# Two products in strict turn, and new start addresses for one half of the weights: a float32 decoder on one Trainium2 core

## The chip, the cores and the metric

The kernel runs on one core of a Trainium2 chip. The metric is the device time of one execution in microseconds. TensorE multiplies, VectorE and ScalarE prepare weights and finish results, GpSimd adds a few tensors, SyncE issues the transfers.

## The reference

Two layers; each takes a sequence of 256 positions by 2048 channels. Cut to the products that matter:

```python
h = jnp.einsum('bsd,dc->bsc', x, w_in)          # 12,288 columns for two branches, 12 + 4,096 for gates
out_a = dilated_mixture(rope(qa), rope(ka), va)  # 12 heads of 128
up_a = jnp.einsum('bsw,wd->bsd', out_a * jax.nn.silu(za), w_up_a)
out_b = forgetting_attention(qb, kb, vb, log_f)  # 12 heads of 128
up_b = jnp.einsum('bsw,wd->bsd', out_b * jax.nn.silu(zb), w_up_b)
g_a, g_b = sigmoid(g_logit + b_gate)             # 2 x 2048 columns
y = jnp.einsum('bsd,de->bse', g_a * up_a + g_b * up_b, w_out)
x = layer_norm(DEEPNORM_ALPHA * x + y, ln_g, ln_b)
```

All is float32. Nearly all arithmetic is in the products with `w_in`, `w_up_a`, `w_up_b` and `w_out`.

## The kernel before

**Split products.** A float32 operand is split into a high part, rounded by ScalarE to the shorter format `float32r`, and a low part, the rest, which VectorE subtracts (`split`, lines 69 and 70). A product is then high x high + high x low + low x high. Activations lie as tiles [128, 2, 256]: for each 128 channels the high part of the 256 positions and behind it the low part. Where the weights stand still in TensorE (`stat_mm`), one 128 x 128 weight tile needs two products:

- a *wide* one, line 164: the weights' high part stands, and 512 columns move (activations high and low), into both halves of a PSUM tile;
- a *narrow* one, line 162: the weights' low part stands, and 256 columns move (activations high).

`fold` adds the two halves of the PSUM tile later. Each product has a weight load of its own, which TensorE makes while the product before it streams. Products for V (`v_mm`, lines 353 and 355) are the other way round: activations stand, 512 and then 256 columns of weights move.

**Units, pieces and order.** A `Unit` is one column block of 128 (or 256 for V) over all 16 or 12 blocks of channels; it is cut into `Piece`s of eight or six such blocks (four for V). `prep` loads a piece's weights, takes one of six buffers `w` and splits into it; it is called four pieces ahead (`prep_to(done + 4)`). `run(i, part)` issues one product, `part` 0 wide and 1 narrow. The loop at the end of `trunk` goes through the pieces in a fixed order: at the start of each layer four units go side by side (five pieces each in the first layer, two in the second), in all other places a piece at a time. In a single piece all wide products come first and then all narrow ones; side by side it is two wide, two narrow. Between units the products of the attention are put in, at fixed places.

**Addresses.** A buffer `w` has 2,240 float32 per partition (8,960 bytes, 35 times 256) and starts at a multiple of 256 bytes, as the activations do. Of 128-wide weights the high part starts 48 elements in and the low part 1,088 elements behind it, so both lie at 192 modulo 256 bytes; a weight tile is 512 bytes a partition, which keeps that. V's weights start 16 elements in, at 64.

`keep_warm` (line 139) is a product of zeros, put in where TensorE has to wait for the layer norm; its weights are the first 128 columns of what it streams.

Of the kernel before, what the change touches and what calls it, by code (L numbers as in the profile page):

```python
# [32 lines left out]
SCALE = HD ** -0.5  # L33

SLOT = KT // 4 * (NV + HEADS)

W_PART = (SLOT + 63) // 64 * 64
W_OFF = 48
V_OFF = 16
# [3 lines left out]
def trunk(ctx: ExitStack, tc: tile.TileContext, xt, w_st, w_v, w_vf, w_up, w_o,  # L43
          b_f, b_g, ln_g, ln_b, rope_c, bias_a, mask_c, ident_c, yt):
    nc = tc.nc
# [17 lines left out]
    def load_raw(ap, n):  # L63
        t = wp.tile([128, SLOT], F32, name="raw", tag="raw", bufs=7)
        nc.sync.dma_start(t[:, :n], ap)
        return t[:, :n]

    def split(hi, lo, src):
        nc.scalar.activation(hi, src, AF.Copy)  # L69
        nc.vector.tensor_tensor(lo, src, hi.bitcast(F32), op=ALU.subtract)  # L70

    class Piece:
# [6 lines left out]
        def prep(self):  # L79
            n = len(self.kts) * self.w  # L80
            raw = load_raw(self.ap, n)
            t = wp.tile([128, 2 * W_PART + 64], F32R, name="w", tag="w", bufs=6)
            o = W_OFF if self.w == 128 else V_OFF
            self.t = t[:, o:o + 2 * W_PART].rearrange("p (a b) -> p a b", a=2)
            split(self.t[:, 0, :n], self.t[:, 1, :n], raw)

        def run(self, i, part):
            s = slice(i * self.w, (i + 1) * self.w)
            self.unit.mm(self.kts[i], self.t[:, :, s], part)

    class Unit:

# [63 lines left out]
    def stat_mm(acts, ps, kt_n, halves=2):  # L156

        def mm(kt, w, part):
            a = acts(kt)
            first, last, o = kt == 0, kt == kt_n - 1, ps()[:, :S]  # L160
            if part == 1:
                nc.tensor.matmul(o, w[:, 1], a[:, 0], start=False, stop=last)  # L162
            elif halves == 2:
                nc.tensor.matmul(ps(), w[:, 0], a, start=first, stop=False)  # L164
            else:
                nc.tensor.matmul(o, w[:, 0], a[:, 0], start=first, stop=False)
                nc.tensor.matmul(o, w[:, 0], a[:, 1], start=False, stop=False)
        return mm

    def fold(dst, ps, scale=1.0):  # L170
# [460 lines left out]
    n = 0  # L631
# [9 lines left out]
    def prep_to(n):  # L641
        nonlocal started
        while started < min(n, len(todo)):
            p = todo[started]
            if p.unit is units[0]:
                load_x(p.kts[0], 2)
            p.prep()
            if p.unit is units[SIDE - 1] and len(p.kts) > 2:
                load_x(p.kts[2], 2)
            started += 1  # L650
            if started == SIDE * len(units[0].pieces) + 1:
                load_rope()
            if started == SIDE * len(units[0].pieces) + 4:
                load_consts()

    done = 0
    for g in order:
        done += len(g)
        n = number[id(g[0].unit)]
        if g[0].first and n in norms:  # L660

            stats, apply = norms[n]
            stats()
            stages = [apply(j2, j2 < 2) for j2 in range(KT // 2)]
            run = [stages[0][0], stages[0][1], stages[1][0]]
            for j2 in range(2, KT // 2):
                run += [stages[j2][0], stages[j2 - 1][1]]
            run.append(stages[-1][1])
            ins = None
            for i, f in enumerate(run):  # L670
                if i == 9:
                    with tc.issue_after(ins.ins):
                        prep_to(done + 2)
                if ins is None:
                    ins = f()
                else:
                    with tc.issue_after(ins.ins):
                        ins = f()
        prep_to(done + 4)
        for p in g:  # L680
            if p.first:
                for f in jobs.get(number[id(p.unit)], []):
                    f()
                if p.unit.before:
                    p.unit.before()
        if len(g) > 1:
            for i in range(0, len(g[0].kts), 2):
                for p in g:
                    for part in range(2):
                        p.run(i, part)  # L690
                        p.run(i + 1, part)
        else:

            for part in range(2):
                for i in range(len(g[0].kts)):
                    g[0].run(i, part)
        for p in g:
            if p.last and p.unit.after:
                p.unit.after()
# [87 lines left out]
```

## Time and profile before

| | |
|---|---|
| median of 3 runs | 1979.7 us (1979.55 to 1981.81) |
| the profiled execution | 1979.52 us |
| its span, first to last instruction | 1977.7 us |
| mean granted TensorE clock | 0.996 of 2.4 GHz |
| TensorE products busy | 99% of the span |
| VectorE, ScalarE, GpSimd busy | 64%, 50%, 4% |
| transfers | 362.74 MB, mean 183 GB/s |

A record of a product is longer than the distance from its start to the next one's, since products are pipelined. So a row with eight products in it is read by its start and the next row's start, and a mean duration is compared with other durations only.

### The profile page before, as it was taken

Reading aid. Unit: us, or ns where it says so; the run is one execution under the profiler, and the core shown is the slowest. Engines: PE = TensorE matmul, PEld = TensorE weight load, DVE = VectorE, ACT = ScalarE, POOL = GpSimd, SP = SyncE. Lnnn points to the kernel's source line nnn. Section 1 sums busy time; section 2 is a strip of 40 time slices with the busy share of each in tenths; the row PEclk is TensorE's granted clock in tenths of the full one; section 3 lists DMA queues with packets and bytes.
Section 4 is the critical chain, followed back from the end, with each engine's and each line's share of the span. In section 5 each row is a group of like instructions: output and inputs, shape, how many; then the busy total and the mean of one; then the engine's idle time right before and its main releaser. Section 6 shows DMA issues by size and latency. Waiting matters only on the chain.

```text
span 1977.7 us, 29731 instructions
## 1 busy us (share of the span) xinstructions
PE 1957.8 (99%) x11449; PEld 1727.2 (87%) x11449; DVE 1269.8 (64%) x1908; ACT 987.3 (50%) x1558; POOL 69.5 (4%) x64
## 2 busy tenths in 40 slices
PE   9999999999999999999999999999999999999997
PEld 7888888889888888888888888888898888888886
DVE  7666665555555555668787666655555555556686
ACT  6444444444544445555465444445454444445544
POOL 0000000001000000001100000000010000000022
PEclk9999999999999999999999999999999999999998
DMA  9655555666656556665555555556666665556651
GB/s 307 204 180 179 172 169 172 192 197 211 185 178 183 179 170 180 183 202 192 160 181 171 179 176 178 166 181 185 203 203 185 185 179 179 170 174 191 210 184 64
DMA packets 108630, 362.74 MB, mean 183 GB/s; under 512 B 12464, under 2 KB 15944, under 8 KB 108488
## 3 DMA queue, kind: packets, MB, share of 16 engines
q1 hardware_dynamic: 107320, 357.42, 58.5%
q0 software_dynamic: 1024, 3.17, 0.7%
q8 instruction: 89, 1.46, 0.3%
q14 instruction: 53, 0.43, 0.1%
q10 hardware_dynamic: 144, 0.26, 0.1%
HBM read 358.68 MB, written 2.12 MB: 182 GB/s over the span
## 4 chain that ended last, share of the span: by engine, by line
PE 98%; DVE 1%; DMA 0%; ACT 0%; issue 0%; DVEq 0%; ACTq 0%
PE mm L164 53%; PE mm L162 27%; PE mm L353 8%; PE mm L355 4%; PE ps_s L258 1%; PE po L287 1%; PE pt L278 1%; PE po L288 1%; PE ps_s L257 1%; PE mm L351 0%; PE mm L348 0%; PE mm L349 0%; DMA xraw<-xt 0%; DVE gated L566 0%; DMA raw<-w_st 0%
## 5 line engine op out<-in xcount | busy, mean ns | idle before, releaser
L70 DVE TENSOR_TENSOR w<-raw,w 128x1024 fp32r<-128x1024 f32 (+3 forms) x716 | 840.5, 1178 | 443.5 <-ACT w L69 442.1
L69 ACT ACTIVATE w<-raw 128x1024 fp32r<-128x1024 f32 (+3 forms) x716 | 717.9, 1004 | 455.5 <-issue 222.6
L164 PE MATMUL mm<-x,w 128*128 128x512 f32 x3328 | 851.2, 396 | 6.4 <-DVE x L589 3.1
L164 PEld LDWEIGHTS mm<-x,w 128*128 128x128 f32 x3328 | 594.3, 188 | 109.9 <-ACT x L577 2.7
L162 PEld LDWEIGHTS mm<-x,w 128*128 128x128 f32 x3328 | 454.0, 188 | 39.2 <-DVE w L70 1.4
L162 PE MATMUL mm<-x,w 128*128 128x256 f32 x3328 | 463.8, 279 | 0.0
L173 ACT ACTIVATE c<-mm 128x256 f32<-128x256 f32 x320 | 120.3, 384 | 456.2 <-PE mm L162 422.5
L175 DVE TENSOR_TENSOR p<-mm,c 128x256 f32<-128x256 f32 x252 | 106.8, 425 | 186.9 <-ACT c L173 186.4
L164 PE MATMUL mm<-gated,w 128*128 128x512 f32 x768 | 196.6, 391 | 0.0
L353 PE MATMUL mm<-w,x 128*128 128x512 f32 x704 | 176.7, 393 | 0.0
L164 PEld LDWEIGHTS mm<-gated,w 128*128 128x128 f32 x768 | 135.3, 188 | 21.1
L353 PEld LDWEIGHTS mm<-w,x 128*128 128x128 f32 x704 | 126.1, 188 | 22.7
L164 PE MATMUL mm<-merged,w 128*128 128x512 f32 x480 | 120.1, 392 | 0.0
L162 PEld LDWEIGHTS mm<-gated,w 128*128 128x128 f32 x768 | 108.3, 188 | 10.4
L162 PE MATMUL mm<-gated,w 128*128 128x256 f32 x768 | 111.2, 279 | 0.0
L355 PEld LDWEIGHTS mm<-w,x 128*128 128x128 f32 x704 | 94.7, 188 | 7.4
L164 PEld LDWEIGHTS mm<-merged,w 128*128 128x128 f32 x480 | 86.0, 188 | 15.5 <-DVE merged L70 0.5
L355 PE MATMUL mm<-w,x 128*128 128x256 f32 x704 | 96.5, 279 | 0.0
L162 PEld LDWEIGHTS mm<-merged,w 128*128 128x128 f32 x512 | 68.1, 188 | 4.8
L162 PE MATMUL mm<-merged,w 128*128 128x256 f32 x512 | 69.9, 279 | 0.0
L447 POOL TENSOR_TENSOR u<-x 128x512 f32<-128x512 f32 x16 | 31.7, 1982 | 603.9 <-DVE merged L70 242.4
L267 ACT ACTIVATE z<-z,s 128x128 f32<-128x128 f32 x96 | 42.3, 444 | 0.0
(128 smaller groups left out, 910.9 us busy)
## 6 DMA issues: line engine op xcount, KB each, us to landing
raw<-w_st SPq DMA_DIRECT2D x408, 512.0 KB, 3.9
raw<-w_up SPq DMA_DIRECT2D x128, 384.0 KB, 3.1
raw<-w_v SPq DMA_DIRECT2D x88, 512.0 KB, 4.4
raw<-w_o SPq DMA_DIRECT2D x64, 512.0 KB, 4.1
raw<-w_vf SPq DMA_DIRECT2D x8, 536.0 KB, 4.4
raw<-w_st SPq DMA_DIRECT2D x12, 256.0 KB, 5.6
nb<-cum POOLq DMA_DIRECT2D x12, 256.0 KB, 4.5
yt<-gated SPq DMA_DIRECT2D x8, 256.0 KB, 2.1
```

The source lines that it names most:

```text
L69: nc.scalar.activation(hi, src, AF.Copy)
L70: nc.vector.tensor_tensor(lo, src, hi.bitcast(F32), op=ALU.subtract)
L162: nc.tensor.matmul(o, w[:, 1], a[:, 0], start=False, stop=last)
L164: nc.tensor.matmul(ps(), w[:, 0], a, start=first, stop=False)
L173: nc.scalar.activation(c, ps[:, S:], AF.Copy, scale=scale)
L175: nc.vector.tensor_tensor(dst, ps[:, :S], c, op=ALU.add)
L257: nc.tensor.matmul(ps[:, 0], q[:, :128], k[:, :128], start=True, stop=True)
L258: nc.tensor.matmul(ps[:, 1:3].rearrange("p a b -> p (a b)"), q[:, 128:], k, start=True, stop=True)
L267: nc.scalar.activation(z[:, sl], z[:, sl], AF.Exp, scale=-1.0, bias=s4[:, c:c + 1], accum_out=s4[:, 2 + c:3 + c])
L353: nc.tensor.matmul(o, xh, w, start=first, stop=False)
L355: nc.tensor.matmul(o[:, :NV], xl, w[:, 0], start=False, stop=last)
L447: nc.gpsimd.tensor_tensor(u, x[:, :, 0], x[:, :, 1], op=ALU.add)
```

## The change

Two things change for weights that stand still. The order within a piece: after each wide product comes the narrow one of the same weights, in single pieces and where four units go side by side. And the addresses: the high part stays at 48 elements (192 modulo 256 bytes), the low part starts at element 1,088 of the buffer (0 modulo 256 bytes) and no longer at 1,136. V's products keep order and addresses.

```diff
@@ Piece @@
             t = wp.tile([128, 2 * W_PART + 64], F32R, name="w", tag="w", bufs=6)
-            o = W_OFF if self.w == 128 else V_OFF
-            self.t = t[:, o:o + 2 * W_PART].rearrange("p (a b) -> p a b", a=2)
-            split(self.t[:, 0, :n], self.t[:, 1, :n], raw)
+            if self.w == 128:
+                self.parts = t[:, W_OFF:W_OFF + n], t[:, W_PART:W_PART + n]
+                split(*self.parts, raw)
+            else:
+                self.t = t[:, V_OFF:V_OFF + 2 * W_PART].rearrange("p (a b) -> p a b", a=2)
+                split(self.t[:, 0, :n], self.t[:, 1, :n], raw)
 
         def run(self, i, part):
             s = slice(i * self.w, (i + 1) * self.w)
-            self.unit.mm(self.kts[i], self.t[:, :, s], part)
+            w = [p[:, s] for p in self.parts] if self.w == 128 else self.t[:, :, s]
+            self.unit.mm(self.kts[i], w, part)
@@ the loop over the pieces @@
             for i in range(0, len(g[0].kts), 2):
                 for p in g:
-                    for part in range(2):
-                        p.run(i, part)
-                        p.run(i + 1, part)
+                    for j in (i, i + 1):
+                        for part in range(2):
+                            p.run(j, part)
         else:
 
-            for part in range(2):
-                for i in range(len(g[0].kts)):
-                    g[0].run(i, part)
+            n = range(len(g[0].kts))
+            for i, part in ([(i, part) for i in n for part in range(2)] if g[0].w == 128 else
+                            [(i, part) for part in range(2) for i in n]):
+                g[0].run(i, part)
```

In `stat_mm`, `w[:, 0]` and `w[:, 1]` become `w[0]` and `w[1]`; the products are the same.

On TensorE, in the second layer, a single piece of eight channel blocks that follows the scores of a head stands like this before (x_81 to x_84 are the activations of two blocks each; 128x512 is a wide product, 128x256 a narrow one):

```order
L258 MATMUL ps_s<-k,q 128x256
L164 MATMUL mm<-x_81,w 128x512 x2
L164 MATMUL mm<-x_82,w 128x512 x2
L164 MATMUL mm<-x_83,w 128x512 x2
L164 MATMUL mm<-x_84,w 128x512 x2
L162 MATMUL mm<-x_81,w 128x256 x2
L162 MATMUL mm<-x_82,w 128x256 x2
L162 MATMUL mm<-x_83,w 128x256 x2
L162 MATMUL mm<-x_84,w 128x256 x2
```

The first eight products of the same piece after the change (lines 164 and 162 are now 169 and 167):

```order
L263 MATMUL ps_s<-k,q 128x256
L169 MATMUL mm<-x_81,w 128x512
L167 MATMUL mm<-x_81,w 128x256
L169 MATMUL mm<-x_81,w 128x512
L167 MATMUL mm<-x_81,w 128x256
L169 MATMUL mm<-x_82,w 128x512
L167 MATMUL mm<-x_82,w 128x256
L169 MATMUL mm<-x_82,w 128x512
L167 MATMUL mm<-x_82,w 128x256
```

The first narrow product moved from the ninth place of the piece to the second, and each kind now stands behind the other.

Where four units go side by side, at the start of the second layer behind the last product of `keep_warm`, TensorE has before:

```order
L139 MATMUL pw<-warm 128x512
L164 MATMUL mm<-x_81,w 128x512 x3
L162 MATMUL mm<-x_81,w 128x256 x2
L164 MATMUL mm<-x_81,w 128x512
L162 MATMUL mm<-x_81,w 128x256 x2
L164 MATMUL mm<-x_81,w 128x512 x2
L162 MATMUL mm<-x_81,w 128x256 x2
```

and after the change:

```order
L144 MATMUL pw<-warm 128x512
L169 MATMUL mm<-x_81,w 128x512
L167 MATMUL mm<-x_81,w 128x256
L169 MATMUL mm<-x_81,w 128x512
L167 MATMUL mm<-x_81,w 128x256
L169 MATMUL mm<-x_81,w 128x512
L167 MATMUL mm<-x_81,w 128x256
```

Here the first narrow product moved from behind three wide ones to behind one. On VectorE, GpSimd and SyncE nothing moved; on ScalarE one split of weights stands one place earlier, ahead of one fold.

## Rows read from the trace of the kernel before

**Rows 1.** The page: busy time by engine, and the last chain's shares by line.

```profile
PE 1957.8 (99%) x11449; PEld 1727.2 (87%) x11449; DVE 1269.8 (64%) x1908; ACT 987.3 (50%) x1558; POOL 69.5 (4%) x64
...
PE mm L164 53%; PE mm L162 27%; PE mm L353 8%; PE mm L355 4%; PE ps_s L258 1%; PE po L287 1%; PE pt L278 1%; PE po L288 1%; PE ps_s L257 1%; PE mm L351 0%; PE mm L348 0%; PE mm L349 0%; DMA xraw<-xt 0%; DVE gated L566 0%; DMA raw<-w_st 0%
```

**Rows 2.** L164, L162: span, PE, PEld, clock, DMA; by source: duration min/median/max ns.

```profile
0.00:1977.80 1977.80, 1167.81 (x4576) 815.50 (x4576) 1.00 0.60 183
...
0.00:1977.80 1977.80, 644.99 (x4608) 630.43 (x4608) 1.00 0.60 183
...
L353 PE MATMUL mm<-w,x x704: 388/394/398, 35.3 to 1703.0; 128*128 128x512 f32 x176
...
L355 PE MATMUL mm<-w,x x704: 276/279/283, 37.2 to 1704.0; 128*128 128x256 f32 x176
```

**Rows 3.** Timeline of TensorE, 790 to 826 us: start, length, line, shape, count.

```profile
790.45 2.00 PE L164 MATMUL mm<-x,w 128*128 128x512 f32 x8
792.28 1.07 PE L162 MATMUL mm<-x,w 128*128 128x256 f32 x8
793.19 1.99 PE L164 MATMUL mm<-x,w 128*128 128x512 f32 x8
795.01 1.11 PE L162 MATMUL mm<-x,w 128*128 128x256 f32 x8
795.96 1.53 PE L164 MATMUL mm<-gated,w 128*128 128x512 f32 x6
...
798.04 1.53 PE L164 MATMUL mm<-gated,w 128*128 128x512 f32 x6
...
823.63 2.00 PE L164 MATMUL mm<-x,w 128*128 128x512 f32 x8
```

**Rows 4.** Groups of TensorE by line, 792.60 to 793.10 us: busy us, mean ns.

```profile
L162 PE MATMUL mm<-x,w 128*128 128x256 f32 x7 | 1.0, 276 | 0.0
```

**Rows 5.** The same, where a narrow run begins: at 792.33, 795.06, 758.69 us.

```profile
L164 PE MATMUL mm<-x,w 128*128 128x512 f32 x1 | 0.4, 394 | 0.0
L162 PE MATMUL mm<-x,w 128*128 128x256 f32 x1 | 0.3, 276 | 0.0
...
L164 PE MATMUL mm<-x,w 128*128 128x512 f32 x1 | 0.4, 392 | 0.0
L162 PE MATMUL mm<-x,w 128*128 128x256 f32 x1 | 0.3, 283 | 0.0
...
L164 PE MATMUL mm<-gated,w 128*128 128x512 f32 x1 | 0.4, 388 | 0.0
L162 PE MATMUL mm<-gated,w 128*128 128x256 f32 x1 | 0.3, 279 | 0.0
```

**Rows 6.** The same, where a wide run begins: at 793.21 and 796.00 us.

```profile
L162 PE MATMUL mm<-x,w 128*128 128x256 f32 x2 | 0.4, 276 | 0.0
L164 PE MATMUL mm<-x,w 128*128 128x512 f32 x1 | 0.4, 388 | 0.0
...
L162 PE MATMUL mm<-x,w 128*128 128x256 f32 x2 | 0.4, 280 | 0.0
L164 PE MATMUL mm<-gated,w 128*128 128x512 f32 x1 | 0.4, 392 | 0.0
```

**Rows 7.** The same, ahead of V's products: at 709.40 and 709.68 us.

```profile
L162 PE MATMUL mm<-x,w 128*128 128x256 f32 x3 | 0.5, 279 | 0.0
...
L353 PE MATMUL mm<-w,x 128*128 128x512 f32 x1 | 0.4, 396 | 0.0
L162 PE MATMUL mm<-x,w 128*128 128x256 f32 x1 | 0.3, 277 | 0.0
```

**Rows 8.** The same, of keep_warm at 980.30 us.

```profile
L139 PE MATMUL pw<-warm 128*128 128x512 f32 x1 | 0.4, 398 | 0.0
```

**Rows 9.** Waits of PEld and of ACT: us in total, times, longest.

```profile
PEld mm L162 <- DVE w L70: 1.4, 4, 0.4
...
ACT w L69 <- PE mm L162: 104.8, 98, 2.7
```

More of the change, by code (lines that the diff above doesn't have):

```diff
@@ L161, in mm @@
             if part == 1:
-                nc.tensor.matmul(o, w[:, 1], a[:, 0], start=False, stop=last)
+                nc.tensor.matmul(o, w[1], a[:, 0], start=False, stop=last)
             elif halves == 2:
-                nc.tensor.matmul(ps(), w[:, 0], a, start=first, stop=False)
+                nc.tensor.matmul(ps(), w[0], a, start=first, stop=False)
             else:
-                nc.tensor.matmul(o, w[:, 0], a[:, 0], start=first, stop=False)
-                nc.tensor.matmul(o, w[:, 0], a[:, 1], start=False, stop=False)
+                nc.tensor.matmul(o, w[0], a[:, 0], start=first, stop=False)
+                nc.tensor.matmul(o, w[0], a[:, 1], start=False, stop=False)
         return mm
```

## The prediction

> **What bounds the kernel now.** I read the page from the top. TensorE's matmul row is busy 1957.8 of 1977.7 us and its weight-load row 1727.2 us, while VectorE is at 64% and ScalarE at 50%; in the chain that ended last line 164 (the wide products) holds 53% of the span and line 162 (the narrow ones) 27% [rows 1]. So what counts is the distance from one product's start to the next one's, and nothing else unless TensorE is made to wait. The sums by line then say how many products there are: 4,576 wide and 4,608 narrow with weights standing still, and 704 of each in the products with moving weights, which the change leaves as they are [rows 2].
>
> A busy TensorE need not be at its peak, so I read distances next, from the starts of runs in a stretch without attention [rows 3]. From 790.45 to 823.63 us there are six pieces of 8 + 8 and eight of 6 + 6 products, 96 pairs in 33.18 us: **345.6 ns for a pair** of one wide and one narrow product. The reader is to see in the same rows that runs of eight narrow products come in two lengths: 792.28 to 793.19 is 0.91 us, 113.8 ns each, and 795.01 to 795.96 is 0.95 us, 118.8 ns each. Wide runs take 1.83 us, 228.8 ns each. The granted clock is 1.00 of 2.4 GHz in the mean [rows 2], at which 512 and 256 columns would stream in 213.3 and 106.7 ns, so each product carries 7 to 16 ns on top.
>
> The records' durations show this more finely than starts to 10 ns: the seven narrow records of the fast run have a mean of 276 ns [rows 4], so a narrow record is some 162.5 ns longer than the distance it stands for (276 against 113.8, rounded), and a wide one 163 (392 [rows 5] against 228.8). With weights standing still I find wide records of 388, 392 and 394 ns [rows 5]; where weights move, wide ones go from 388 to 398 and narrow ones from 276 to 283 [rows 2]. In distances: wide 225.5 to 235.5, narrow 113.5 to 120.5.
>
> Which of these levels a product takes is handed on by the product before it. Behind a wide of 394 ns the first narrow takes 276; behind one of 392 it takes 283; behind one of 388 it takes 279 [rows 5]. Behind a narrow of 276 the first wide takes 388, behind one of 280 it takes 392 [rows 6]. In between, a narrow run keeps its level, as the mean of the seven shows [rows 4].
>
> **The change, part by part.** *Removed and added work:* none. Products, loads, splits and transfers are the same in number and size; each product's weight load still runs under the product before it.
>
> *The order.* Before, of the 16 loads of a piece of eight, seven high and one low part are loaded under wide products, seven low and one high (the next piece's) under narrow ones. After, every low part is loaded under a wide product and every high part under a narrow one, and each wide is followed by a narrow and the reverse. So what [rows 5, 6] show decides at every product and no longer once in eight. With the loads at the addresses of before, I can walk the chain from those rows: narrow 276, wide 388, narrow 279, wide 392, narrow 283, and then wide 392 and narrow 283 again and again, if a 283 hands on what a 280 does. That is (392 - 163) + (283 - 162.5) = 349.5 ns a pair, 3.9 more than now. The order by itself is worth 4,576 x 3.9 = +17.8 us.
>
> *The addresses.* The activations start at 0 modulo 256 bytes, high and low parts both at 192 before; now the low part starts at 0. It is the part that is loaded under the wide product. A load at 0 under a wide product of this kind is in no row. The nearest rows: at the start of a unit with moving weights the activations become the loaded operand, at 0, under the last narrow product. That product takes 277 ns at two such places (566.7 and 709.5 us), where the three before it at the second have a mean of 279 [rows 7]: two ns faster, so the position of a load counts, and 0 is better there, though the wide product behind it is one of 396 [rows 7]. The other row goes against it: a keep-warm product, 512 columns wide, whose next load has the same start as its moving operand takes 398 [rows 8], the slowest level, but it stands right behind a restart and the load reads the very bytes that it streams. The bounds of the wide product are then 388 and 398 ns, so the pair lies between 225.5 + 113.5 = 339.0 and 235.5 + 120.5 = 356.0 ns: from -30.2 to +47.6 us over 4,576 pairs.
>
> I take the narrow row as nearer (the same activations, in mid-stream) and let it bring the wide to within 1.5 ns of its fastest level: 227 ns. A wide a little above 388 must then leave its narrow at 276 and not at 279, which would repeat itself: 227 + 113.5 = 340.5 ns, 5.1 less than now. That is 4,576 x 5.1 = **-23.3 us**.
>
> The Trainium skill speaks against this term ("SBUF — State Buffer", section on two separate sides): it gives TensorE ports of its own that wait for nobody, with a second independent read port for weight loads, so that no start address would matter. The narrow record of 277 disagrees; by the rule this term would be 0.
>
> *Low parts needed sooner.* In a single piece the first low product comes seven wides (1.6 us) earlier, in the groups of four units one wide (0.23 us) earlier. In the single pieces this is hidden: ScalarE's split waited 98 times on a narrow product of TensorE [rows 9], that is for one of the six weight buffers to come free, so splits are done pieces ahead, and a piece is 2.1 to 2.8 us long [rows 3]. Were that cover gone, every piece would pay 1.6 us. In the groups of four the cover is thin: weight loads of line 162 waited four times for VectorE's low part, 1.4 us together [rows 9]. Each of the four pays up to 0.23 us more: +0.9 us. At most all 20 + 8 pieces of such groups pay it, 6.4 us. One split moves ahead of one fold on ScalarE in the first group; both have slack, nothing.
>
> *Sum.* The profiled execution took 1979.5 us (span 1977.7), the median of the three runs is 1979.7. 1979.5 - 23.3 + 0.9 = **1957.1 us**. VectorE, ScalarE and the transfers would go up by 1% of their shares and stay covered.
>
> **Rivals.**
> *The address does nothing for the wide product, the order does its part (slower).* Place: every pair. For it: the walk through [rows 5, 6], whose loads all lie at 192, ends in the slow pair, and the one wide product with an aligned load is slow [rows 8]. Against it: the 277 ns records. Price +17.8 + 0.9: 1998 us. It decides once the narrow product behind a wide keeps to 283 and not to 276; with a wide at 394 on top it would be 1979.5 + 4,576 x 6.4 + 0.9 = 2010.
> *Neither matters.* Place: every pair again, if fast and slow levels keep taking turns as they do now. For it: in the mean over 96 pairs all levels come up, in runs of six as in runs of eight [rows 3]. Against it: the levels are not random, one follows from the one before [rows 5, 6], and a strict turn has one way from each. Price 0 to +0.9: 1980 us. By the rule of the Trainium skill's page on SBUF above, it would go this way too.
> *Half a gain.* Two levels take turns, as 340.5 and 345.6: 343 ns, 1968.5 us. It counts with my forecast.
>
> **How the numbers follow.** The forecast with the half gain has 0.56, the slower rival 0.28, no change 0.16. The forecast's own range is 1949 (the lower bound, 1979.5 - 30.2) to 1970. The range for 8 in 10 must hold the middle case and most of the slower one: 1949 to 1998. A measurement of this kernel tells about 0.2% (4 us) from no change: faster 0.56, same 0.16, slower 0.28.
>
> **What would show it.** The same stretch would hold its 96 pairs in 32.7 us (340.5 ns) and not 33.18. Narrow records of the line that was 162 would have 276 to 277 as median and wide ones 388 to 390; 283 and 392 would show the slower rival, 279 and 392 the neutral one. Products with moving weights must stay at 393 and 279 ns, or something else moved. In the first 18 us, waits of weight loads for VectorE would be more than four, and over 2.3 us together if the groups of four pay. I am wrong if the levels are set by something that the load's address doesn't touch: then the whole sum turns on the chain of levels, and that one ends slow.

## The result, and the profile after

| | before | after |
|---|---|---|
| median, side by side on one chip, 4 runs each | 1979.62 us | 1965.72 us (1965.15 to 1966.0) |
| ratio | | **0.9926** [0.9913, 0.9938] |
| span of the profiled execution | 1977.7 us | 1963.9 us |
| mean granted TensorE clock | 0.996 | 0.996 |

The kernel became 14 us faster, where 22.6 us were forecast. First the page after: busy time of TensorE, and the last chain's shares by line.

```profile
PE 1942.3 (99%) x11449; PEld 1718.4 (87%) x11449; DVE 1269.5 (65%) x1908; ACT 987.8 (50%) x1558; POOL 69.7 (4%) x64
...
PE mm L169 52%; PE mm L167 27%; PE mm L358 8%; PE mm L360 4%; PE ps_s L263 1%; PE po L292 1%; PE pt L283 1%; PE po L293 1%; PE ps_s L262 1%; PE mm L356 0%; PE mm L353 0%; PE mm L354 0%; DMA raw<-w_st 0%; DVE gated L571 0%; DVE w L71 0%
```

The bound is the same as in [rows 1]: TensorE, 99% busy, with the same lines (169 wide and 167 narrow, 358 and 360 for V). The products' own time shrank by 15.5 us (1957.8 to 1942.3).

The stretch that the prediction measured in [rows 3] begins now at 784.87 us, with the same 96 pairs. Timeline of TensorE after: start, length, line, shape, count.

```profile
784.87 0.39 PE L169 MATMUL mm<-x,w 128*128 128x512 f32 x1
785.10 0.28 PE L167 MATMUL mm<-x,w 128*128 128x256 f32 x1
785.21 0.39 PE L169 MATMUL mm<-x,w 128*128 128x512 f32 x1
...
817.51 0.39 PE L169 MATMUL mm<-x,w 128*128 128x512 f32 x1
```

From 784.87 to 817.51 us are 32.64 us, **340.0 ns a pair**, where 340.5 were forecast and 345.6 stood before. So here the change did what was said of it. The durations by source agree (minimum/median/maximum in ns, first and last start):

```profile
L169 PE MATMUL mm<-x,w x3328: 387/389/747, 5.8 to 1843.0; 128*128 128x512 f32 x196
L169 PE MATMUL mm<-gated,w x768: 389/389/389, 314.1 to 1859.3; 128*128 128x512 f32 x192
...
L167 PE MATMUL mm<-x,w x3328: 276/276/415, 6.5 to 1843.2; 128*128 128x256 f32 x196
L167 PE MATMUL mm<-gated,w x768: 276/276/278, 314.3 to 1859.5; 128*128 128x256 f32 x192
...
L358 PE MATMUL mm<-w,x x704: 388/392/394, 35.6 to 1691.6; 128*128 128x512 f32 x176
...
L360 PE MATMUL mm<-w,x x704: 276/278/283, 37.4 to 1692.7; 128*128 128x256 f32 x176
```

Wide records of 389 and narrow ones of 276 ns are the medians that were forecast, and all 768 wide products of `gated` have exactly 389. V's products are a shade shorter than in [rows 2].

What the medians hide is in the timeline behind the attention's transposes (line 283, `flip`). The same columns, after:

```profile
58.83 0.49 PE L283 MATMUL pt<-ident,z 128*128 128x128 f32 x3
59.08 0.48 PE L169 MATMUL mm<-x,w 128*128 128x512 f32 x1
59.39 0.28 PE L167 MATMUL mm<-x,w 128*128 128x256 f32 x1
59.51 0.40 PE L169 MATMUL mm<-x,w 128*128 128x512 f32 x1
59.74 0.28 PE L167 MATMUL mm<-x,w 128*128 128x256 f32 x1
59.86 0.40 PE L169 MATMUL mm<-x,w 128*128 128x512 f32 x1
...
64.64 0.28 PE L167 MATMUL mm<-x,w 128*128 128x256 f32 x1
64.76 0.59 PE L292 MATMUL po<-pts,v 128*128 128x256 f32 x2
```

From 59.51 to 64.76 us are 15 pairs in 5.25 us: **350.0 ns a pair**, in the same kernel, at the same addresses modulo 256 bytes, in the same order. Nothing waits there. A stretch that runs at 350.0 pair after pair stays at it until other work or a wait comes in between. Over all starts of the timeline there are 4,446 distances from one wide product over one narrow to the next wide: 3,326 are at most 342 ns, 909 lie between 348 and 353, the other 211 lie outside both, are the long first pair behind other work, or hold a wait. Of the 909, 644 are in 46 such stretches of 15 pairs behind transposes (the last pair of each runs into other work and isn't counted), and 186 follow V's first unit of the second branch and the transposes of its forget gate, 93 in each layer.

Last the waits, in us, times and longest: of weight loads in the first 18 us and of TensorE's products in the whole after, and of its products in the whole before.

```profile
PEld mm L169 <- ACT w L70: 2.5, 3, 1.3
...
PEld mm L167 <- DVE w L71: 1.1, 2, 0.6
...
PE mm L169 <- DVE x L594: 4.4, 3, 2.4
...
PE mm L167 <- DVE w L71: 0.5, 2, 0.3
```

```profile
PE mm L164 <- DVE x L589: 3.1, 2, 2.4
```

Weight loads wait 1.1 us in two for VectorE's low part, less than the 1.4 us in four of [rows 9]. The products themselves wait 0.5 us in two for it, and before they had no such wait. They wait 1.3 us more for the layer norm's result, in one wait more.

### The profile page after: what moved, and what is told of

The parts are those of the page before. It is cut to its first block, busy times and chain, and to the rows that moved or that the text cites. A ratio compares the mean times of both kernels' runs of the same rounds, so it can differ in the third digit from the quotient of the medians.

```text
span 1963.9 us, 29732 instructions
## 1 busy us (share of the span) xinstructions
PE 1942.3 (99%) x11449; PEld 1718.4 (87%) x11449; DVE 1269.5 (65%) x1908; ACT 987.8 (50%) x1558; POOL 69.7 (4%) x64
## 4 chain that ended last, share of the span: by engine, by line
PE 97%; DVE 1%; DMA 1%; ACT 1%; issue 0%; DVEq 0%; ACTq 0%
PE mm L169 52%; PE mm L167 27%; PE mm L358 8%; PE mm L360 4%; PE ps_s L263 1%; PE po L292 1%; PE pt L283 1%; PE po L293 1%; PE ps_s L262 1%; PE mm L356 0%; PE mm L353 0%; PE mm L354 0%; DMA raw<-w_st 0%; DVE gated L571 0%; DVE w L71 0%
## 5 line engine op out<-in xcount | busy, mean ns | idle before, releaser
L169 PE MATMUL mm<-x,w 128*128 128x512 f32 x3328 | 1162.8, 395 | 7.5 <-DVE x L594 4.4
L167 PE MATMUL mm<-x,w 128*128 128x256 f32 x3328 | 924.0, 278 | 0.5 <-DVE w L71 0.5
L169 PEld LDWEIGHTS mm<-x,w 128*128 128x128 f32 x3328 | 625.9, 188 | 140.4 <-issue 3.6
L167 PEld LDWEIGHTS mm<-x,w 128*128 128x128 f32 x3328 | 625.9, 188 | 2.0 <-DVE w L71 1.1
L169 PE MATMUL mm<-gated,w 128*128 128x512 f32 x768 | 262.5, 389 | 0.0
L167 PE MATMUL mm<-gated,w 128*128 128x256 f32 x768 | 212.0, 276 | 0.0
L169 PEld LDWEIGHTS mm<-gated,w 128*128 128x128 f32 x768 | 144.2, 188 | 30.0
L169 PE MATMUL mm<-merged,w 128*128 128x512 f32 x480 | 164.4, 391 | 0.1
L358 PEld LDWEIGHTS mm<-w,x 128*128 128x128 f32 x704 | 125.9, 188 | 22.6
L167 PEld LDWEIGHTS mm<-gated,w 128*128 128x128 f32 x768 | 144.2, 188 | 0.0
L167 PE MATMUL mm<-merged,w 128*128 128x256 f32 x512 | 141.6, 277 | 0.0
L169 PEld LDWEIGHTS mm<-merged,w 128*128 128x128 f32 x480 | 90.1, 188 | 19.3 <-DVE merged L71 0.8
L167 PEld LDWEIGHTS mm<-merged,w 128*128 128x128 f32 x512 | 96.1, 188 | 0.1
L452 POOL TENSOR_TENSOR u<-x 128x512 f32<-128x512 f32 x16 | 31.7, 1980 | 597.1 <-DVE merged L71 239.6
```

Of the source, the lines that this page charges most:

```text
L167: nc.tensor.matmul(o, w[1], a[:, 0], start=False, stop=last)
L169: nc.tensor.matmul(ps(), w[0], a, start=first, stop=False)
L358: nc.tensor.matmul(o, xh, w, start=first, stop=False)
L452: nc.gpsimd.tensor_tensor(u, x[:, :, 0], x[:, :, 1], op=ALU.add)
```

## The experiments

Theory A, the prediction's: each product takes one of a few levels, set by where the load under it and the operand that it streams start, and by the product before it. The turn makes one sequence of levels repeat, and the addresses choose which. Its rivals: one of the two edits does it alone (B the order, C the address), neither counts, or the rest of the loss is waits and not levels. Each kernel is an edit of the changed one (the last two of the tenth) and was run against the kernel before on the same chip.

**1. The order alone** (low part back at 192).

```diff
-                self.parts = t[:, W_OFF:W_OFF + n], t[:, W_PART:W_PART + n]
+                self.parts = t[:, W_OFF:W_OFF + n], t[:, W_PART + 48:W_PART + 48 + n]
```

> The strict turn of the change, with both parts at 192 modulo 256 bytes as before. Theory A (a product's level follows from the one before it and from where the next load lies): the chain of the rows of before ends in wide 392, narrow 283, 349.5 ns a pair, 1998 us; with the slow pair of the profile after (232.5 + 117.5) it would be 350 ns, 2000 us. Theory B (the gain is the order's): 1966 us, as with the change. Theory C (it is the address's): 1980 us, as before.

Measured: 2001.15 us, ratio 1.0105 [1.0088, 1.0122]. The walk through [rows 5, 6] gave 349.5 ns a pair and 1998 us. The time of theory A was hit; the pair that it had walked to was not. Durations of the products of `gated`, minimum/median/maximum:

```profile
L169 PE MATMUL mm<-gated,w x768: 392/392/396, 318.8 to 1892.3; 128*128 128x512 f32 x192
...
L167 PE MATMUL mm<-gated,w x768: 278/280/283, 319.1 to 1892.5; 128*128 128x256 f32 x192
```

Wide 392 and narrow 283 again and again would be 392 and 283 throughout. In the timeline three pairs repeat instead: 392 and 278, 396 and 280, 392 and 283, at 347, 351 and 349 ns. Behind attention there is a second sequence of 353.3 ns in the mean, with 1,776 of the 4,330 pairs.

**2. The addresses alone** (low part at 0, the order of before).

```diff
-                    for j in (i, i + 1):
-                        for part in range(2):
-                            p.run(j, part)
+                    for part in range(2):
+                        p.run(i, part)
+                        p.run(i + 1, part)
...
+            for part in range(2):
+                for i in range(len(g[0].kts)):
+                    g[0].run(i, part)
```

> The order of before (runs of wide, then runs of narrow), with the low part at 0 modulo 256 bytes. Now seven of eight low loads lie under narrow products. Theory A: narrow products with a load at 0 take 277 ns by record (114.5 ns of distance) and no longer 116.8 in the mean, wide ones stay as they were with their loads at 192: -2.3 ns for 7 of 8 pairs, -9 us, 1971 us, and the fast pair of 340 ns doesn't last. Theory B: 1980 us. Theory C: 1966 us.

Measured: 1993.83 us, ratio 1.0064 [1.0049, 1.0079]. A miss: I had expected a gain. Each edit alone loses, 20.8 and 12.7 us by the ratios, and together they gain 14. In the long stretch of the table below wide products take 230.5 ns and narrow ones 118.2, both slower than before (228.9 and 116.5). So a load at 0 is no better under a narrow product, though I had read from [rows 7] that it is.

**3 and 4. Other places for the low part**, at 64 and at 128, in strict turn.

```diff
-                self.parts = t[:, W_OFF:W_OFF + n], t[:, W_PART:W_PART + n]
+                self.parts = t[:, W_OFF:W_OFF + n], t[:, W_PART + 16:W_PART + 16 + n]
...
+                self.parts = t[:, W_OFF:W_OFF + n], t[:, W_PART + 32:W_PART + 32 + n]
```

> The strict turn, high part at 192, low part at 64 modulo 256 bytes. Theory A: another start address gives another chain of levels; it settles between 339 and 356 ns a pair, 1950 to 2028 us, and not where 0 does; I lean to slower than the change, 1980 us. Theory B: 1966 us, the address is without effect.

> The strict turn, high part at 192, low part at 128 modulo 256 bytes. Theory A: again a chain of its own between 339 and 356 ns a pair; I lean to slower than the change, 1985 us. Theory B: 1966 us.

Measured: 2003.56 us, ratio 1.0115 [1.01, 1.013], and 1986.34 us, ratio 1.0025 [1.0015, 1.0036]. For both I had leaned to something slower than the change, 1980 and 1985 us; the first came out 24 us slower than that. The place of the low part by itself moves the time by 38 us between the best (0) and the worst (64).

**5 and 6. Other places for the high part.** In the first both lie at 0, in the second the high part is at 0 and the low one at 192, the change's two places exchanged.

```diff
-                self.parts = t[:, W_OFF:W_OFF + n], t[:, W_PART:W_PART + n]
+                self.parts = t[:, :n], t[:, W_PART:W_PART + n]
...
+                self.parts = t[:, :n], t[:, W_PART + W_OFF:W_PART + W_OFF + n]
```

> The strict turn, both parts at 0 modulo 256 bytes: only the load under the narrow product differs from the change. Theory A: the run with only the low part moved showed that a load at 0 under narrow products in a row costs (119 to 120 ns); the pair settles slow, narrow 120 and wide 229, about 349 ns, 2000 us. If only the wide product's load mattered, the fast pair would stay: 1966 us.

> The strict turn with the two addresses exchanged: high parts at 0 (loaded under narrow products), low parts at 192 (loaded under wide ones). Theory A (each kind of product has its own good address): slow, like the strict turn with both at 192 or worse, 350 to 355 ns a pair, 2000 to 2024 us. If the difference between the two parts' addresses is what matters and not which lies where: 1966 us.

Measured: 2005.04 us, ratio 1.012 [1.0105, 1.0135], and 1988.67 us, ratio 1.0039 [1.0024, 1.0054]. The first came out near the 2000 us expected, but not in the way expected: narrow products were to take 120 and wide ones 229 ns, and in the table below they take 117.2 and 236.1. The exchange was expected to cost more than it did; the sign was right. With the low part at 0 as in the change, the first is one of the two slowest kernels: 0 for the low part is good beside a high part at 192, not in itself.

**7 and 8. Is it the distance between the two?** In the change the low part lies 64 bytes behind the high one, modulo 256. Two more pairs with that distance:

```diff
-                self.parts = t[:, W_OFF:W_OFF + n], t[:, W_PART:W_PART + n]
+                self.parts = t[:, :n], t[:, W_PART + 16:W_PART + 16 + n]
...
+                self.parts = t[:, 32:32 + n], t[:, W_PART + 48:W_PART + 48 + n]
```

> The changed kernel with the high part at 0 and the low part at 64 modulo 256 bytes: the low part lies 64 bytes behind the high one, as in the change (192 and 0). Theory D (what counts is how far apart the two loads start, modulo 256): the long stretch behind 330 us at 340.0 ns a pair and the whole at 1960 to 1970 us. Rival L (the low part must start where the moving activations start, at 0; or the high part must be at 192): 346.7 to 353.3 ns as in the runs that had one of the two elsewhere, 1986 to 2005 us.

> The changed kernel with the high part at 128 and the low part at 192 modulo 256 bytes, again 64 bytes apart. Theory D: 340.0 ns a pair behind 330 us, 1960 to 1970 us. Rival L: 346.7 to 353.3 ns, 1986 to 2005 us.

Measured: 1985.78 us, ratio 1.0028 [1.0016, 1.004], and 1988.7 us, ratio 1.0044 [1.0027, 1.0061]. Theory D (that the distance of the two loads counts) falls.

All of them in one table. The pair is the distance from the first start to the last start of a wide product between 330 and 430 us, over the pairs between them (after: 330.07 to 429.69 us, 293 pairs); no attention lies there, and the clock is 1.00.

| high, low (modulo 256) | order | wide, narrow ns | pair ns | ratio to before |
|---|---|---|---|---|
| 192, 192 | before | 228.9, 116.5 | 345.0 | 1 |
| 192, 0 | before | 230.5, 118.2 | 349.9 | 1.0064 |
| 192, 192 | turn | 230.0, 118.9 | 348.9 | 1.0105 |
| **192, 0** | turn | 226.9, 113.1 | **340.0** | 0.9926 |
| 192, 64 | turn | 236.0, 117.4 | 353.3 | 1.0115 |
| 192, 128 | turn | 228.3, 118.3 | 346.7 | 1.0025 |
| 0, 0 | turn | 236.1, 117.2 | 353.3 | 1.012 |
| 0, 192 | turn | 233.3, 113.3 | 346.7 | 1.0039 |
| 0, 64 | turn | 229.5, 117.1 | 346.7 | 1.0028 |
| 128, 192 | turn | 231.0, 115.7 | 346.7 | 1.0044 |

The same stretch in windows, with the wide products after and with the low part at 64: us, PE busy (count), PEld busy (count), granted clock, share and GB/s of transfers.

```profile
330.00:430.00 100.00, 100.00 (x295) 55.23 (x295) 1.00 0.64 191
```

```profile
330.00:430.00 100.00, 100.00 (x284) 52.92 (x283) 1.00 0.62 185
```

In 100 us at full clock, without a wait, 11 pairs fewer go through. In the rows of 192, 192 and of 0, 0 in turn, three pairs repeat and not one (347, 351, 349 and 350, 360, 350 ns). No single address explains the table: a narrow product is at 113 with high and low at 192 and 0 and also with the two exchanged, a wide one at 227 with the low part at 0 beside 192 but at 236 beside 0.

**9. What stands ahead: another order of the attention's pieces.** `flip` ahead of `values`, so that in one place a transpose is no longer the last product ahead of a piece.

```diff
-                    [lambda: values(0), lambda: flip(1)],
+                    [lambda: flip(1), lambda: values(0)],
```

> The changed kernel, with the transposes of head 1 ahead of the value products of head 0 and no longer behind them. In the trace of the changed kernel 46 stretches of 15 pairs at 350 ns begin right behind transposes, and what follows value products or scores falls into the pair of 340 ns within three pairs. Theory A (the products before a piece set the level into which it falls): the 23 or so pieces that now begin behind value products go fast, 23 x 15 x 10 ns = 3.5 us less, 1962.3 us, and their stretches are gone from the trace. Rival D (the slow stretch belongs to that piece, its buffers and tiles): 1965.8 us, the stretches stay.

Measured: 1962.58 us, ratio 0.991 [0.9894, 0.9927]. The stretches of 15 pairs at 350 fell from 46 to 24, the pairs between 348 and 353 ns from 909 to 721; 3.1 us less than the changed kernel's median, 3.4 expected. The size was hit and the place missed. The pieces behind `values` were to become fast and those behind `flip` alone to stay slow. It is the other way round: all 24 pieces behind `flip` alone are fast now, and the 24 behind `flip` and `values` stayed at 350. Behind the first of each:

```profile
59.78 0.49 PE L283 MATMUL pt<-ident,z 128*128 128x128 f32 x3
...
61.17 0.39 PE L169 MATMUL mm<-x,w 128*128 128x512 f32 x1
61.39 0.28 PE L167 MATMUL mm<-x,w 128*128 128x256 f32 x1
61.51 0.39 PE L169 MATMUL mm<-x,w 128*128 128x512 f32 x1
...
66.35 0.38 PE L293 MATMUL po<-pts,v 128*128 128x128 f32 x2
...
66.92 0.40 PE L169 MATMUL mm<-x,w 128*128 128x512 f32 x1
67.16 0.28 PE L167 MATMUL mm<-x,w 128*128 128x256 f32 x1
67.27 0.40 PE L169 MATMUL mm<-x,w 128*128 128x512 f32 x1
```

The pair at 61.17 us takes 0.34 us, the one at 66.92 us 0.35. Up to 65.4 us this kernel and the changed one have the same products and weight loads in the same order, and still the piece at 60 us runs at 340 here and at 350 there. So theory A, as it was put, missed here. Rival D of this expectation (the slow stretch belongs to the piece) falls too. The 3.1 us don't show that the order of the products ahead picks the sequence.

**10. The transposes' identity 64 bytes further on.** The order stays; the last thing streamed ahead of such a stretch, the identity matrix, starts elsewhere. Its tile grows by 256 bytes with it, so tiles that lie behind it may have moved by that much; whether this counts, no run shows.

```diff
     def const_tile(ap, name):
+        if name == "ident":
+            return const.tile([128, 192], F32, name=name)[:, 16:144]
         return const.tile(list(ap.shape), F32, name=name)
```

> The changed kernel, with the identity of the transposes 64 bytes further on in its own tile; no other address changes modulo 256. Theory A: the transposes end at another point, so the pieces behind them enter in another way: the stretches of 15 slow pairs behind transposes go (46 x 15 x 10 ns = 6.9 us less, 1959 us) or grow in number (some 1969 us); the shares of fast pieces behind scores and values stay. Rival D: 1965.8 us, stretches as before.

Measured: **1957.8 us**, ratio 0.9882 [0.9868, 0.9897], the fastest kernel here; it beats the changed one too (their intervals don't meet). The same place in its timeline, two lines further on in the code:

```profile
58.50 0.49 PE L285 MATMUL pt<-ident,z 128*128 128x128 f32 x3
58.74 0.48 PE L171 MATMUL mm<-x,w 128*128 128x512 f32 x1
59.06 0.28 PE L169 MATMUL mm<-x,w 128*128 128x256 f32 x1
59.18 0.39 PE L171 MATMUL mm<-x,w 128*128 128x512 f32 x1
59.41 0.28 PE L169 MATMUL mm<-x,w 128*128 128x256 f32 x1
59.53 0.39 PE L171 MATMUL mm<-x,w 128*128 128x512 f32 x1
59.75 0.28 PE L169 MATMUL mm<-x,w 128*128 128x256 f32 x1
59.87 0.39 PE L171 MATMUL mm<-x,w 128*128 128x512 f32 x1
60.09 0.28 PE L169 MATMUL mm<-x,w 128*128 128x256 f32 x1
```

The first pair, from 59.18 to 59.53, still takes 0.35 us; from there it is 0.34 (59.53 to 59.87). Of the 46 stretches none is left: all 48 pieces behind transposes are fast. Pairs at 350 fall from 909 to 340. The weights, their places in the buffers and their order are those of the changed kernel. The mean over all distances below 370 ns goes from 342.26 to 340.89, 1.37 x 4,323 = 5.9 us. The profiled execution has besides no fall of the clock where the changed kernel's had one (below), worth some 1.7 us: 7.6 of the 8.8 us between the spans of the two (1963.9 and 1955.1).

**11 and 12. The same for V's products.** On the tenth version, V in strict turn, first with addresses after the pattern of the change (the low part at 0, the high part at 64, the wide product streaming low, then high), then with V's addresses as they were. The core of the first:

```diff
-                self.t = t[:, V_OFF:V_OFF + 2 * W_PART].rearrange("p (a b) -> p a b", a=2)
-                split(self.t[:, 0, :n], self.t[:, 1, :n], raw)
+                self.t = t[:, :2 * (W_PART + V_OFF)].rearrange("p (a b) -> p a b", a=2)
+                split(self.t[:, 1, :n], self.t[:, 0, :n], raw)
...
-            for i, part in ([(i, part) for i in n for part in range(2)] if g[0].w == 128 else
+            for i, part in ([(i, part) for i in n for part in range(2)] if g[0].w in (128, NV) else
```

> The version with the identity moved, and in it the 704 V pairs go strictly in turn as well, with V's low parts at 0 and its high parts at 64 modulo 256 bytes (the wide product streams low, then high; the narrow one high). Theory A (a pair's level is set by what stands ahead and by the start addresses of loads and moving rows): V pairs go from about 344.5 ns (228.7 and 115.7) to 340.0, 704 x 4.5 ns = 3.2 us off 1957.8, some 1954.6 us. Rival B (V has its own levels, or order and addresses only tell on the 128-wide slots): 1957.8 us, no difference. A loss would say that the relation does not carry over to moving weights with still activations.

> The version with the identity moved, and V products strictly in turn with V's addresses as they are. Theory A: the turn without the addresses costs V what it cost the rest, about 350 ns a pair for 344.5, 704 x 5.5 ns = 3.9 us more, some 1961.7 us. Rival B: 1957.8 us, no difference.

Measured: 1961.59 us, ratio 0.9905 [0.9892, 0.9919], and 1964.05 us, ratio 0.9916 [0.9903, 0.993]. Groups by line of the tenth version, of the one with addresses, of the one without (busy us, mean ns):

```profile
L360 PE MATMUL mm<-w,x 128*128 128x512 f32 x704 | 175.5, 391 | 0.0
...
L362 PE MATMUL mm<-w,x 128*128 128x256 f32 x704 | 95.8, 278 | 0.0
```

```profile
L352 PE MATMUL mm<-w,x 128*128 128x512 f32 x704 | 246.6, 394 | 0.0
...
L353 PE MATMUL mm<-w,x 128*128 128x256 f32 x704 | 195.4, 278 | 0.0
```

```profile
L352 PE MATMUL mm<-w,x 128*128 128x512 f32 x704 | 249.4, 395 | 0.0
...
L353 PE MATMUL mm<-w,x 128*128 128x256 f32 x704 | 198.4, 282 | 0.0
```

The turn without addresses costs V 4 + 4 ns a pair, 704 x 8 = 5.6 us, where theory A had 3.9. The pattern of the change did not carry over: 3 ns lost by the records (2.1 us; by the starts 3.8 ns, 2.7 us) and not 4.5 gained. Not all that the two lose to the tenth version is V's. In each of them, 201 pairs of the output products run at 350 in one layer and at 340 in the other, the first layer in the one and the second in the other, which is 2.0 us; the tenth version has both at 340. The products ahead are the same in both layers. And the profiled execution of the version with addresses, the longest of its four, has two short falls of the granted clock around the layer norm. Windows of it, and of the tenth version: us, PE busy (count), clock, transfers.

```profile
975.00:985.00 10.00, 7.55 (x35) 0.83 0.00 1
...
1000.00:1010.00 10.00, 8.07 (x38) 0.83 0.75 245
```

```profile
975.00:985.00 10.00, 8.80 (x50) 1.00 0.00 0
...
1000.00:1010.00 10.00, 8.22 (x46) 1.00 0.78 250
```

A mean of 0.83 over 10 us is a third of it at 1.2 GHz and the rest at 2.4, and costs about 1.7 us; each fall begins within 1.2 us behind a wait of TensorE of 1.9 to 2.5 us at the turn of the layers. The tenth version waited 1.93 us there too, at 1001.78 us, and had no fall. The kernel before and the changed one had one such fall each, so between these two it takes nothing from the comparison.

## Why the prediction was right in sign, and where a third of the gain went

**What bounds the kernel** was right: TensorE is still 99% busy, and all of the gain is in distances between products.

**The order, +17.8 us,** was right in sign and near in size, 20.8 us alone, but the walk that gave the size was wrong. It let each record settle the next one and ended in wide 392 and narrow 283 for good. In the first kernel the same wide 392 is followed by a narrow 278 and by a 283, and a wide 396 stands in the cycle, which no row showed. One sequence is 348.9 ns a pair in the mean, the other 353.3, all pairs 350.7; that 349.5 lies so near is luck. The kernel before could have warned: within a run its wide records go 388, 392, 394 and round again, and only the narrow run of [rows 4] keeps one level; the slow one goes 283, 280, 279. The rival that made the order the whole effect was a sound one: it is what happens with the low part at 192.

**The addresses, to -23.3 us in sum,** is the term that was mis-sized. Where it works the pair is 340.0 ns for 340.5, with records of 389 and 276 as said. The step that failed is "a wide a little above 388 must then leave its narrow at 276 and not at 279, which would repeat itself": it does repeat itself, but it isn't the only sequence that does. 233 and 117 ns repeat as well, and which one a stretch falls into is settled in its first pairs. The prediction said that a strict turn has one way from each level; it had read hand-ons in [rows 5, 6] and could have asked where the chain starts anew, which it does behind every piece of attention. Of 4,446 distances 909 were in the other sequence: (350.0 - 340.5) x 909 = 8.6 us given back, and -23.3 + 8.6 = -14.7. That the gain went there is shown by the tenth kernel, which has 340 such pairs and is 7.9 us faster with the same weights and order. What picks the sequence is not shown. Moving the identity turned all 46 stretches; but the ninth kernel turned pieces with nothing changed right ahead of them, and the 201 output pairs of the last two kernels go either way behind the same products. The mean over all pairs below 370 ns, 342.3, is that of the prediction's half gain (343 ns, 1968.5 us), reached in another way: whole stretches at one pair or the other, and not the two by turns.

The ground that I gave for the term was weak, and that its 340.5 ns came out was luck. I took the narrow record of 277 in [rows 7] as a sign that a load at 0 is better. The second, fifth and sixth kernels contradict that: at 0 a load can be the worst place (353.3 ns with both there). What decides is the combination of both loads and the order (the start of the streamed activations was never moved), and of eight combinations in strict turn this one alone holds 340. The trace of before had no row for it. The working is also loose by half a nanosecond: it takes 163 ns off a wide record in the order's term and 162.5 in the bounds, which is 2.3 us over 4,576 pairs.

**The Trainium skill's rule** ("SBUF — State Buffer", section on two separate sides), that TensorE's ports wait for nobody, would, as the prediction applied it, have made all these kernels the same. They span 340.0 to 353.3 ns a pair and 1965.72 to 2005.04 us with addresses alone. The rows don't show where in the engine or the memory the difference arises, so whether it is a port at all stays open.

**Low parts needed sooner, +0.9 us,** was paid in part: the weight loads' waits for VectorE fell from 1.4 to 1.1 us, but the products' own rose from nothing to 0.5 us, in two waits for four expected. Products waited 1.3 us more for the layer norm, which no term had.

**V's products** were to stay and gained a little: by the starts, 1.9 us over 704 pairs. They start behind other levels now; I had not thought of it.

**The sum.** Distances under 260 ns behind wide products and under 140 behind narrow ones have means of 229.2 and 116.6 before, 228.1 and 114.4 after. With the longer ones, which hold the waits, all distances behind wide products add up to 1063.2 us before and 1058.0 after, those behind narrow ones to 541.0 and 534.2: 5.2 and 6.8 us less. With V's 1.9 that is the 13.9 us by which the span shrank, before rounding.

**What stays open:** why 192 and 0 go together; what picks one of the two sequences, for which a place in memory or the exact moment at which a stretch begins was tested in no run; and why the 186 pairs behind V's first unit of the second branch and its forget gate's transposes stay at 350 even in the tenth version, though these transposes use the moved identity too. With the pairs elsewhere, most of them where a layer begins, 340 remain, 340 x 10 = 3.4 us that nobody has got back.

## What to carry to other kernels

Where TensorE is busy all the time and every product has a load of its own, the distance between two starts is a level that repeats, not a constant: measure it in a long undisturbed stretch, then look for stretches in the same kernel that sit on another level, and at how they begin. Start addresses of the loaded operands and the order of products work together, so try them together: here each edit alone lost 13 and 21 us and the pair of them gained 14. Don't carry an address pattern over to products of another kind without a run: the one that won here lost 2 to 3 us on V. And when a time comes out as expected, look whether it changed in the place where it should: the ninth kernel's did not.

## What the runs showed of the hardware

- In strict turn a pair of 512 and 256 columns of the 4-byte `float32r` has means of 340.0, 346.7, 348.9 or 353.3 ns in the long stretch, by the places of the two loads, and 350.0 ns in the change's second sequence. Such a sequence holds over stretches of 15 to over 290 pairs. In the first and fifth kernels its unit is three pairs (347, 351, 349 and 350, 360, 350 ns), not one.
- Moving a 128-column identity by 64 bytes, in a tile 256 bytes larger, turned 46 stretches of 15 pairs behind its use from 350 to 340 ns a pair, though none of them touches it.
- The same products in the same order can run at 340 or at 350 ns: the first piece behind `flip` in the changed and the ninth kernel, and the 201 output pairs in the two layers of the eleventh and of the twelfth.
- A record's length exceeds the distance that it stands for by 160 to 164 ns in all these kernels, so records compare kernels to some 3 ns, and starts do it better.
